# Hybrid stick-breaking and retention step: four raw operand buffers, three sum buffers, and x rows that wait for products

## The chip, the cores and the metric

One core of a Trainium2 chip runs the whole kernel. The metric is the device time of one execution in microseconds (us); the time of a kernel is the median of its runs. A core has five engines that each take their instructions in order: TensorE (PE, the matmuls), VectorE (DVE), ScalarE (ACT), GpSimd (POOL) and SyncE (SP). DMA transfers are issued from the queues of SP, ACT and POOL, and each issue, too, stands in its engine's order.

## The reference

One layer over 1024 prompt frames and 8 streams of 16 frames each, model width 2048, 8 + 8 heads of 128, in fp32. Cut to what matters:

```python
h = rms_norm(xp, norm_pre)
q_sb, k_sb, v_sb, gate_sb, q_r, k_r, v_r, gate_r = project(h, w_in, pos)   # 2048 -> 8 x 1024
o_sb = stick_breaking(q_sb, k_sb, v_sb)        # causal, per block of 128 queries
o_r, s = retention(q_r, k_r, v_r, s0, log_gamma)   # chunks of 64, carries a state
y = concat(head_rms_norm(o_sb, g_sb) * silu(gate_sb),
           head_rms_norm(o_r, g_r) * silu(gate_r))
out = einsum('bte,ed->btd', y, w_out)          # 2048 -> 2048
xp = xp + rms_norm(out, norm_post)
```

The sample streams run the same with 1024 cached frames of keys and values and a retention state. Returned are the new rows, the keys and values, and the states.

## The kernel before

Every fp32 operand is split into a high and a low part (`split`, L163 to L166: ACT writes the high part, L165, DVE the rest, L166), and every product is three matmuls: high by high, high by low, low by high. The names follow that: `mh`, `ml` for the moving operand, `wh`, `wl` for weights, `ah`, `al` for the left operands of the last stage; `mr`, `wr`, `yr`, `ys`, `br` are raw tiles that a DMA fills.

The 1024 + 128 frames are nine tiles of 128 rows in two groups. Group 0 has four prompt tiles and the sample (640 columns), group 1 the other four (512). The stages in order of time:

1. The normalized, transposed input `h` is made and written to memory (`s_h`) for group 1.
2. Group 0: per head the eight column panels of the input projection (L369, or L425 for the value rows), with stick-breaking attention and retention between them. The gated head outputs go to memory (`s_y`, L687).
3. The change of groups, about 1057 to 1104 us: `load_moving` (L243) reads group 1's operand from `s_h` block by block (16 blocks of 128 x 512, in quarters of four) through raw tiles `mr` and splits it. It is driven from the matmul loops of the last head of group 0 (`gates`, L1123, and `project_rows`, L403), which step it a quarter at a time, while the last attention of group 0 is still going on: `kp`, `kb` and `be` (L632, L633) are its sigmoids on ACT.
4. Group 1, the same, until about 1943 us. In the place of `load_moving`, `first_left` (L1032) reads the first left operands of the last stage from `s_y` and `s_s` through `mr`.
5. The output projection, as seven products of half-size matrices in a Strassen-like scheme (`product(n, nh, ...)`, L1188, matmuls L1162, L1165, L1166). Its left operands are rows of `y` (`s_y`) or sums of them (`s_s`), read by `left` (L293) and `left_sample` (L315); its right operands are blocks of `w_out` or sums of them (`s_b`), read by L1179. `sums` (L274) makes the sums: two loads fill a tile `br`, four DVE operations (L286) combine it, ACT's queue stores it (L289). Product (5, 0) of group 0 runs from 1943 us, product 1 from 1988, products 2, 5, 3, 6, 7 follow, then (4, 0).
6. The last product, (4, 1): `keep_blocks` (L1375) loads and splits all its weight blocks once; four tiles, `LAST`, are multiplied one after the other, normalized, added to the rows of x that `load_row` (L1336) has read, and stored (L1289).

What sets the order: matmuls are written out in sequence, and after each block `tick()` lets the jobs around it go a step. A `Job` is a generator; what it yields is the number of ticks until its next step (`D_MR`, `D_OP`, `D_SUM3` are such numbers). So the program's text and these numbers fix the order on every engine and queue. An instruction whose operand is not there holds up everything behind it on its engine. A raw tile with two buffers can be asked for again only after the split before the last has read it, and SP, which issues the load, waits for that, with all later loads behind it.

Of the kernel before, what the change touches and what calls it, by code (L numbers as in the profile page):

```python
# [11 lines left out]
F32 = mybir.dt.float32  # L12
# [47 lines left out]
D_MR = 6  # L60
D_OP = 2
D_SUM2 = (4, 6, 36)
D_SUM3 = (2, 3, 6)
LAG = 2
AHEAD = 2
HT = KT // 2
# [24 lines left out]
def tile_hybrid_step(  # L91
# [150 lines left out]

    def load_moving(mov, at, n, src):  # L243
        hi, lo = mov
        for k in range(KT):
            q, j = divmod(k, WQ)
            if q == len(hi):
                for x, y in zip(mov, moving_part(mp, NMAX, q)):
                    x.append(y)
            r = wp.tile([P, n], F32, name="mr", tag="mr", bufs=2)  # L250
            nc.sync.dma_start(r, src(k))
            split(hi[q][:, j, at : at + n], lo[q][:, j, at : at + n], r)
            yield D_MR

    def sum_weights(k, c):
# [15 lines left out]
        ops = ((3, 1, 3, "a"), (1, 0, 1, "s"), (0, 3, 0, "s"), (2, 2, 0, "s"))  # L271
        return load, ops, s_s[gi][h]

    def sums(pool, items, pace):  # L274

        def fetch(load):
            r = pool.tile([P, 4, 256], F32, name="br", tag="br", bufs=2)
            load(r)
            return r

        r = fetch(items[0][0])
        yield pace[2]
        for i, (_, ops, dst) in enumerate(items):
            nxt = fetch(items[i + 1][0]) if i + 1 < len(items) else None
            for o, a, b, how in ops:
                pin(nc.vector.tensor_tensor(r[:, o], r[:, a], r[:, b], ALU.add if how == "a" else ALU.subtract))  # L286
                yield pace[0]
            yield pace[1]
            pin(nc.scalar.dma_start(dst, r))  # L289
            r = nxt  # L290
            yield pace[2]
# [147 lines left out]
    with ExitStack() as s1:  # L439
# [592 lines left out]
        def first_left():  # L1032
            drain(summed[0])
            mine["s", 0] = [[half[h // WQ][:, h % WQ, NB_TOK:] for h in range(HT)] for half in mov]
            yield from left_sample(0, *mine["s", 0], wp, "mr", 2)
            mine[0, 5] = kept(0)
            yield from left(0, 5, *mine[0, 5], wp, "mr", 2)

        ret_job = sb_job = sub = loads = after = None
        for gi, g in enumerate(GROUPS):  # L1040
# [7 lines left out]
            for h in range(H):  # L1048
# [28 lines left out]
                def attention():  # L1077
                    nonlocal sb_job, sub, ip
                    acc = project(g, mov, col(0, h))
                    held = project(g, mov, col(1, h)) if h == H - 1 else None  # L1080
                    drain(sb_job)
                    if gi == 1 and h == 0:
                        drain(sub)
                        late.close()
                        banks.append(s1.enter_context(tc.tile_pool(name="psx", bufs=1, space=PSUM)))
                        ip = s1.enter_context(tc.tile_pool(name="ip2", bufs=1))
                        items = [sum_weights(k, c) for k in range(HT) for c in range(4)]
                        items[8:8] = [sum_rows(0, h) for h in range(H)]
                        summed.append(Job(sums(ip, items, D_SUM2), 8))
                        Job(residuals(), 150)  # L1090
                    q2 = [kq.tile([P, NB_TOK], F32R, name=f"q{c}", tag=f"q{c}") for c in "hl"]
                    evac_split(acc, *q2)
                    qs = None
                    if SAMPLE in tiles:
                        qs = kq.tile([P, P], F32, name="qs", tag="qs")
                        nc.scalar.activation(qs, acc[1][0][:, 2 * P : 3 * P], AF.Copy)
                    out = Out(4, "so")
                    rest = rows_in["sb"] = {}
                    if SAMPLE in tiles:
                        drain(sub)  # L1100
                        sub = Job(decode(h, qs, rest), D_DEC)
                    acc = held or project(g, mov, col(1, h))
                    kT = kq.tile([P, NMAX], F32, name="kT", tag="kT")
                    for a, (o, m) in acc:
                        nc.scalar.activation(kT[:, o : o + m], a[:, :m], AF.Copy)
                    pool, n = (ip, PT * P) if gi else (kq, NB_TOK)
                    k2 = [pool.tile([P, n], F32R, name=f"k{c}", tag=f"k{c}") for c in "hl"]
                    evac_split(acc, *k2, off * P)
                    if gi == 1:
                        kp = wp.tile([P, NB_TOK], F32, name="kpast", tag="mr", bufs=2)  # L1110
                        nc.sync.dma_start(kp, s_k[h])
                        split(k2[0][:, :NB_TOK], k2[1][:, :NB_TOK], kp)
                    rest["kT"] = kT
                    sb_job = Job(sb_branch(gi, g, h, out, q2, k2, kT, rest), D_NAT[phase[0]])
                    if h % 2 == 0:
                        pair["s"] = ep.tile([P, 8, 2, P], F32, name="vn", tag="vn")
                        project_rows(g, mov, col(2, h), pair["s"], off)
                    vn = pair["s"][:, :, h % 2, :]
                    if gi == 1:
                        nc.sync.dma_start(vn[:, :4, :], s_v[h])  # L1120
                    rest["vn"] = vn

                def gates():  # L1123
                    nonlocal after, loads
                    if h < H - 1:
                        rows_in["sb"]["sg"] = gate(project(g, mov, col(3, h)), "sg")
                        return

                    after = [[], []]
                    loads = first_left() if gi else load_moving(after, 0, NB_TOK, from_h)  # L1130
                    accs = project_pair(g, mov, (col(7, h), col(3, h)), loads)
                    rows_in["rest"]["rg"], rows_in["sb"]["sg"] = gate(accs[0], "rg"), gate(accs[1], "sg")

# [100 lines left out]
            outs[0, i] = mp.tile([P, WQ * NMAX], F32, name=t, tag=t)  # L1234
        Job(collect(5, 0, accs), 1)
        mine[0, 1] = kept(1)
        nxt = Job(left(0, 1, *mine[0, 1], wp, "mr", 2), D_OP)
        Job(collect(5, 1, product(5, 1, (0,), True, D_OUT)), 1)
        drain(nxt)
        drain(ret_job)  # L1240
# [4 lines left out]
    with ExitStack() as s3:  # L1245
# [68 lines left out]
        def both(n, groups):  # L1314
            made = []
            for g in groups:
                mine[g, n] = operand(c3, ("ah", "al"), 256, bufs=2) if g else kept(at[n])
                made.append(left(g, n, *mine[g, n], rp, f"yr{g}", 4))
            return made

        def jobs_of(made):
# [14 lines left out]
        def load_row(key):  # L1336
            i = LAST.index(key)
            pool, tag = ((xp[0], "x0"), (xp[0], "x1"), (rp, "out0"), (rp, "out1"))[i]
            rows[key] = pool.tile([P, D], F32, name=f"x{i}", tag=tag)
            pin(nc.sync.dma_start(rows[key], x_rows(tile_of((key[0], 2 + key[1])))))  # L1340

        def early_rows():
            for key in LAST[:2]:
# [1 line left out]
                yield 30  # L1345

        (first,) = both(1, G1)
        more = Job(sums(fp, [sum_rows(1, h) for h in range(H)], D_SUM3), 16)
        Job(load_gpost(), 40)
        ready = [Job(left_sample(1, *mine["s", 1], fp, "ys", 4), 24)]  # L1350
        for p in range(4):
# [23 lines left out]
        def keep_blocks():  # L1375
            for k in range(HT):
                wr = wp.tile([P, 512], F32, name="wr3", tag="wr", bufs=5)
                pin(nc.sync.dma_start(wr, weights_of(4, 1, k)))
                yield 1
                pin(*split(keep[0][k], keep[1][k], wr))  # L1380
                yield D_KEEP
            load_row(LAST[2])

        keeping = Job(keep_blocks(), 1)
        Job(collect(4, 0, product(4, 0, BOTH, False, 2)), 1)
# [1 line left out]
        scaled = [c3.tile([P, 2, 512], F32, name=f"og{t}", tag=t) for t in ("sh", "sl")]  # L1387
        for g, p in LAST:
            key = g, 2 + p
            if (g, p) == LAST[0]:  # L1390
                load_row(LAST[3])
            a = bank()
            for k in range(HT):
                times(a, mine[g, 4], k, TS[p], keep[0][k], keep[1][k], k == 0, k == HT - 1, k == 0)
                if (g, p) == (0, 0):
                    tick()
                    tick()
            if (g, p) == (0, 0):
                while jobs:
                    tick()  # L1400
            o = area(key, 1)
            nc.vector.tensor_tensor(o, o, a, ALU.subtract)
            square(key, 1, o)
            t = scaled[g][:, p, :]
            nc.vector.tensor_tensor(t, o, gpost[:, 512:1024], ALU.mult)
            rs = scale(key)
            for c in (0, 2, 3, 1):
                part = t if c == 1 else area(key, c)
                if c or (g, p) == (1, 1):
                    x = rows[g, p][:, c * 512 : (c + 1) * 512]  # L1410
                    nc.vector.scalar_tensor_tensor(part, part, rs, x, ALU.mult, ALU.add)
                    store(key, c, nc.sync, part)
                else:
                    nc.scalar.activation(part, part, AF.Copy, scale=rs)
                    add_out(key, c)
# [104 lines left out]
```

## Time and profile before

| | us |
|---|---|
| median of 3 runs | 2318.3 |
| lowest, highest | 2317.97, 2323.03 |
| profiled execution, its time | 2318.99 |
| profiled execution, span from first to last instruction | 2317.3 |
| PE busy | 2265.7 (98%) |
| DVE busy | 1231.3 (53%) |
| ACT busy | 919.1 (40%) |
| POOL busy | 358.1 (15%) |
| mean share of DMA engines of the three largest queues | 44.6%, 12.1%, 11.8% |

The granted clock of PE is 0.994 of full speed over the span. A row of a timeline has the start in us, the duration in us, the engine, the line of the kernel, the operation, output and inputs with their shapes, and in brackets how long the engine was idle before it, with what ended the idle time. An x2 or x3 behind a row joins equal instructions that follow each other. Matmuls are pipelined: the duration of one is longer than the distance to the next, and the distance tells the speed.

### The profile page before, as it was taken

The numbers are of one execution on the slowest core, as the hardware profiler recorded it, in microseconds if no ns is written. First come the engines' busy times: TensorE is split into PE (matmuls) and PEld (weight loads), VectorE is DVE, ScalarE is ACT, GpSimd is POOL, SyncE is SP. The second block draws the span as 40 slices with busy tenths as digits, with TensorE's granted clock in tenths as the row PEclk, the third lists the DMA queues.
The fourth block names the chain that finished last, engine by engine and source line by source line (L and its number), as shares of the span: only waits on it lengthen the run. The fifth ranks groups of instructions, "written<-read, shape, count | busy, mean of one in ns | idle before, by whom it ended". The sixth has DMA issues, their size and how long they took to land.

```text
span 2317.3 us, 39306 instructions
## 1 busy us (share of the span) xinstructions
PE 2265.7 (98%) x14496; PEld 2046.9 (88%) x14496; DVE 1231.3 (53%) x2541; ACT 919.1 (40%) x1951; POOL 358.1 (15%) x601
## 2 busy tenths in 40 slices
PE   7999999999999999999999999999999999899997
PEld 7999999999999999998888989898888887788886
DVE  7234444354534445355556565655665666546566
ACT  6323333333333333334433433343443445435363
POOL 3002020120202021111102111120211212000020
PEclk9999999999999999999999999999999999999999
DMA  7547657575566657568768777778787767755596
GB/s 257 180 144 201 190 152 218 173 196 186 150 194 198 195 158 231 168 187 254 192 205 233 216 210 236 214 229 230 221 231 216 212 169 182 247 191 183 148 210 177
DMA packets 446497, 462.61 MB, mean 200 GB/s; under 512 B 181984, under 2 KB 309984, under 8 KB 444640
## 3 DMA queue, kind: packets, MB, share of 16 engines
q1 hardware_dynamic: 315952, 295.69, 44.6%
q0 software_dynamic: 28720, 78.41, 12.1%
q10 hardware_dynamic: 101632, 86.00, 11.8%
q8 instruction: 113, 1.85, 0.3%
q14 instruction: 80, 0.66, 0.1%
HBM read 355.12 MB, written 114.29 MB: 203 GB/s over the span
## 4 chain that ended last, share of the span: by engine, by line
PE 85%; DMA 7%; DVE 4%; issue 2%; ACT 2%; SPq 0%; POOL 0%; DVEq 0%; ACTq 0%; POOLq 0%
PE acc L369 46%; PE accn L425 17%; PE a L1166 4%; PE a L1162 4%; PE a L1165 4%; PE pa L750 2%; PE z L720 2%; PE zc L789 1%; PE pd L853 1%; DMA mr<-s_h 1%; DMA s_o<-so 1%; PE pa L898 1%; DVE ml L166 1%; PE pS L913 1%; PE rs L880 1%
## 5 line engine op out<-in xcount | busy, mean ns | idle before, releaser
L369 PE MATMUL acc<-mh,wh 128*128 128x256 f32 (+2 forms) x2304 | 662.6, 340 | 0.0
L369 PE MATMUL acc<-ml,wh 128*128 128x256 f32 (+2 forms) x2304 | 659.0, 339 | 0.0
L369 PE MATMUL acc<-mh,wl 128*128 128x256 f32 (+2 forms) x2304 | 656.6, 338 | 0.0
L166 DVE TENSOR_TENSOR wl<-wr,wh 128x512 fp32r<-128x512 f32 x504 | 346.3, 690 | 495.3 <-ACT wh L165 475.9
L165 ACT ACTIVATE wh<-wr 128x512 fp32r<-128x512 f32 x504 | 317.0, 630 | 653.3 <-PE acc L369 341.1
L369 PEld LDWEIGHTS acc<-ml,wh 128*128 128x128 f32 x2304 | 421.6, 188 | 31.3 <-issue 3.3
L369 PEld LDWEIGHTS acc<-mh,wl 128*128 128x128 f32 x2304 | 424.2, 188 | 27.8
L369 PEld LDWEIGHTS acc<-mh,wh 128*128 128x128 f32 x2304 | 420.1, 188 | 31.9 <-issue 3.3
L425 PE MATMUL accn<-whn,mh 128*128 128x256 f32 x1152 | 330.4, 287 | 0.6 <-DVE rg L452 0.6
L425 PE MATMUL accn<-wln,mh 128*128 128x256 f32 x1152 | 326.4, 283 | 0.0
L425 PE MATMUL accn<-whn,ml 128*128 128x256 f32 x1152 | 326.0, 283 | 0.0
L425 PEld LDWEIGHTS accn<-whn,mh 128*128 128x128 f32 x1152 | 221.4, 192 | 4.0 <-issue 1.1
L425 PEld LDWEIGHTS accn<-wln,mh 128*128 128x128 f32 x1152 | 221.4, 192 | 0.8
L425 PEld LDWEIGHTS accn<-whn,ml 128*128 128x128 f32 x1152 | 221.1, 192 | 0.0
L166 DVE TENSOR_TENSOR wln<-wrn,whn 128x512 fp32r<-128x512 f32 x128 | 87.6, 687 | 147.0 <-ACT whn L165 146.6
L165 ACT ACTIVATE whn<-wrn 128x512 fp32r<-128x512 f32 x128 | 80.6, 633 | 187.7 <-PE accn L425 83.2
L613 POOL DMA_DIRECT2D be<-s_be x128 | 94.2, 742 | 149.8 <-DMA s_be<-be 126.9
L649 DVE TENSOR_TENSOR_SCAN kp<-kp 128x1152 f32<-128x1152 f32 (+4 forms) x40 | 82.8, 2069 | 52.1 <-POOL kp L638 35.4
L638 POOL TENSOR_SCALAR_AFFINE_SELECT kb<-kb 128x128 f32<-128x128 f32 x64 | 30.6, 485 | 459.2 <-ACT kb L632 456.9
L776 POOL DMA_DIRECT2D kcT<-cache_k x64 | 34.6, 545 | 423.6 <-PE pd L853 268.8
L1162 PE MATMUL a<-wh,mh 128*128 128x512 f32 x240 | 94.0, 393 | 2.6 <-ACT wh L165 1.9
L1166 PE MATMUL a<-wh,ml 128*128 128x512 f32 x240 | 94.0, 392 | 0.0
(259 smaller groups left out, 3008.9 us busy)
## 6 DMA issues: line engine op xcount, KB each, us to landing
wr<-w_cols SPq DMA_DIRECT2D x384, 256.0 KB, 4.4
wrn<-w_rows SPq DMA_DIRECT2D x128, 256.0 KB, 3.6
kcT<-cache_k POOLq DMA_DIRECT2D x64, 512.0 KB, 8.2
vc<-cache_v SPq DMA_DIRECT2D x64, 512.0 KB, 5.9
wr<-s_b SPq DMA_DIRECT2D x80, 256.0 KB, 4.2
br<-w_out SPq DMA_DIRECT2D x64, 256.0 KB, 5.0
s_b<-br ACTq DMA_DIRECT2D x32, 512.0 KB, 4.8
wr<-w_out SPq DMA_DIRECT2D x48, 256.0 KB, 3.9
```

The costliest lines, as they stand in the source:

```text
L165: nc.scalar.activation(hi, src, AF.Copy),
L166: nc.vector.tensor_tensor(lo, src, hi.bitcast(F32), ALU.subtract),
L369: last = nc.tensor.matmul(a[:, :m], lhs[:, j, :], rhs[w][:, j, o : o + m], start=(w == 0 and j == 0 and n == 0), stop=(w == KT // WQ - 1 a ...
L425: anchor[0] = nc.tensor.matmul(a, lhs[q][:, jj, ts], rhs[:, j, :], start=(w == 0 and j == 0 and n == 0 and t % 2 == 0), stop=(w == KT // 2 ...
L613: q.dma_start(raw[32 * i : 32 * i + 32, :].rearrange("p (k a) -> p k a", a=32), s[:, :, 32 * i : 32 * i + 32].rearrange("k (j b) a -> b (k ...
L649: nc.vector.tensor_tensor_scan(rev, rev, rev, 1.0, ALU.mult, ALU.bypass)
L720: nc.tensor.matmul(z[:, :c], q2[a][:, i * P : (i + 1) * P], k2[b][:, s : s + c], start=(m == 0), stop=(m == 2),)
L750: nc.tensor.matmul(po[:, :P], at[:, j, :], vn[:, j, :], start=(j == 0), stop=(j == t))
L776: ready.append((kc, nc.gpsimd.dma_start(kc, cache_k[h, m // 4, m % 4])))
L1162: ins = nc.tensor.matmul(a, hi[k][:, ts], wh, start=first, stop=False)
L1165: nc.tensor.matmul(a, hi[k][:, ts], wl, start=False, stop=False)
L1166: anchor[0] = nc.tensor.matmul(a, lo[k][:, ts], wh, start=False, stop=last)
```

## The change

1. Raw `mr` tiles have four buffers (`MR`) instead of two. `load_moving` asks for four blocks first, and for block k + 4 after the split of block k; at the change to group 1 the first four are asked for before the last pair of projections begins. `first_left`, the past keys (`kpast`) and the operand of product (0, 1) use four buffers as well.
2. In the last stage, the left operands of group 0 pass through `mr` instead of a tile `yr0` of their own; those of group 1 keep theirs, now called `yr`.
3. `sums` takes its number of buffers: two for the sums of weights, as before, and three for the sums of group 1's rows. Those start 30 ticks into the last stage instead of 16, and their first pace is 3 instead of 2.
4. `load_row` for the last two rows of x moves from the end of `keep_blocks` and the first of the four tiles to the tiles (0, 0) and (0, 1), and waits for the last product matmul written before it.

```diff
-D_SUM3 = (2, 3, 6)
+D_SUM3 = (3, 3, 6)
+MR = 4
@@ load_moving
+        raw = []
+
+        def load(k):
+            r = wp.tile([P, n], F32, name="mr", tag="mr", bufs=MR)
+            nc.sync.dma_start(r, src(k))
+            raw.append(r)
+
+        for k in range(MR):
+            load(k)
+        yield D_MR
         for k in range(KT):
...
-            r = wp.tile([P, n], F32, name="mr", tag="mr", bufs=2)
-            nc.sync.dma_start(r, src(k))
-            split(hi[q][:, j, at : at + n], lo[q][:, j, at : at + n], r)
+            split(hi[q][:, j, at : at + n], lo[q][:, j, at : at + n], raw.pop(0))
+            if k + MR < KT:
+                load(k + MR)
             yield D_MR
@@ sums
-    def sums(pool, items, pace):
+    def sums(pool, items, pace, bufs):
-            r = pool.tile([P, 4, 256], F32, name="br", tag="br", bufs=2)
+            r = pool.tile([P, 4, 256], F32, name="br", tag="br", bufs=bufs)
@@ first_left
-            yield from left_sample(0, *mine["s", 0], wp, "mr", 2)
+            yield from left_sample(0, *mine["s", 0], wp, "mr", MR)
-            yield from left(0, 5, *mine[0, 5], wp, "mr", 2)
+            yield from left(0, 5, *mine[0, 5], wp, "mr", MR)
@@ sums of the weights
-                        summed.append(Job(sums(ip, items, D_SUM2), 8))
+                        summed.append(Job(sums(ip, items, D_SUM2, 2), 8))
@@ attention
-                        kp = wp.tile([P, NB_TOK], F32, name="kpast", tag="mr", bufs=2)
+                        kp = wp.tile([P, NB_TOK], F32, name="kpast", tag="mr", bufs=MR)
@@ gates
                     loads = first_left() if gi else load_moving(after, 0, NB_TOK, from_h)
+                    if gi == 0:
+                        next(loads)
@@ product (0, 1)
-        nxt = Job(left(0, 1, *mine[0, 1], wp, "mr", 2), D_OP)
+        nxt = Job(left(0, 1, *mine[0, 1], wp, "mr", MR), D_OP)
@@ both
-                made.append(left(g, n, *mine[g, n], rp, f"yr{g}", 4))
+                made.append(left(g, n, *mine[g, n], *((rp, "yr", 4) if g else (wp, "mr", MR))))
@@ load_row
-            pin(nc.sync.dma_start(rows[key], x_rows(tile_of((key[0], 2 + key[1])))))
+            load = nc.sync.dma_start(rows[key], x_rows(tile_of((key[0], 2 + key[1]))))
+            pin(load)
+            if i > 1:
+                tc.add_manual_dep(
+                    load.ins,
+                    anchor[0].ins.name,
+                    mybir.DependencyInfo(mybir.DependencyClass.Sync, mybir.DependencyReason.DATA),
+                    reason="behind the weights",
+                )
@@ sums of group 1's rows
-        more = Job(sums(fp, [sum_rows(1, h) for h in range(H)], D_SUM3), 16)
+        more = Job(sums(fp, [sum_rows(1, h) for h in range(H)], D_SUM3, 3), 30)
@@ keep_blocks
-            load_row(LAST[2])
@@ the last four tiles
-            if (g, p) == LAST[0]:
-                load_row(LAST[3])
+            if g == 0:
+                load_row((1, p))
```

The diff's lines shift those of the functions behind by up to 21: `split` is at L166 and L167, the first stage of `kp` and `be` at L643 and L644.

Three places of the order of instructions. First ACT at the change of groups, the last two quarters of group 1's operand (`mh<-mr`) beside the projection's weights (`whn<-wrn`), the gates (`rg`, `sg`) and the last attention's sigmoids (`kp`, `be`, `kb`). Before:

```order
L165 ACTIVATE mh_12331<-mr 128x512 x2
L165 ACTIVATE whn<-wrn 128x512
L451 ACTIVATE sg<-acc_11996 128x256
L451 ACTIVATE sg<-acc_11997 128x384
L165 ACTIVATE mh_12430<-mr 128x512
L632 ACTIVATE kp<-zc 128x512
L165 ACTIVATE mh_12430<-mr 128x512
L633 ACTIVATE be<-zc 128x512
```

and with the change:

```order
L166 ACTIVATE whn<-wrn 128x512
L462 ACTIVATE sg<-acc_12004 128x256
L462 ACTIVATE sg<-acc_12005 128x384
L166 ACTIVATE mh_12438<-mr 128x512 x4
L643 ACTIVATE kp<-zc 128x512
L644 ACTIVATE be<-zc 128x512
```

Before, a split of the last quarter stands ahead of `kp` and another between `kp` and `be`; the last two come later. With the change all four stand ahead of `kp`, and `be` follows `kp`.

Second DVE in product 1 of the last stage: the last splits of its left operand (`al<-yr`) among splits of weights (`wl<-wr`) and the sums (`br<-br`; the number names the tile, so 21574 is the third sum and 21628 the fourth before, 21552 the second and 21620 the third after). Before:

```order
L286 TENSOR_TENSOR br_21574<-br_21574 128x256
L166 TENSOR_TENSOR wl3_21583<-wr3_21580,wh3_21582 128x512
L166 TENSOR_TENSOR al_21407<-yr1_21495,ah_21406 128x256
L286 TENSOR_TENSOR br_21574<-br_21574 128x256 x2
L166 TENSOR_TENSOR al_21407<-yr1_21545,ah_21406 128x256
L166 TENSOR_TENSOR wl3_21613<-wr3_21610,wh3_21612 128x512
L286 TENSOR_TENSOR br_21574<-br_21574 128x256
```
```order
L286 TENSOR_TENSOR br_21628<-br_21628 128x256
L166 TENSOR_TENSOR wl3_21643<-wr3_21640,wh3_21642 128x512
L166 TENSOR_TENSOR al_21407<-yr1_21586,ah_21406 128x256
```

and with the change:

```order
L297 TENSOR_TENSOR br_21552<-br_21552 128x256
L167 TENSOR_TENSOR al_21407<-yr_21534,ah_21406 128x256
L167 TENSOR_TENSOR wl3_21605<-wr3_21602,wh3_21604 128x512
L297 TENSOR_TENSOR br_21552<-br_21552 128x256 x2
```
```order
L167 TENSOR_TENSOR al_21407<-yr_21578,ah_21406 128x256
L167 TENSOR_TENSOR wl3_21634<-wr3_21631,wh3_21633 128x512
L297 TENSOR_TENSOR br_21620<-br_21620 128x256
```

The last `al` stood behind the first operation of the fourth sum, and now stands behind the second sum and ahead of the third.

Third SP at the end of product (4, 0), with the x rows and the last weight blocks (`wr<-s_b`, L1179 for (4, 0) and L1378 for the last product). Before:

```order
L1179 DMA wr_24111<-s_b_6_109 128x512
L1378 DMA wr_24125<-s_b_7_118 128x512
L1340 DMA x_24132<-x_prompt 128x2048
L1179 DMA wr_24137<-s_b_7_110 128x512
L1340 DMA x_24181<-x_prompt 128x2048
L1289 DMA out<-mh_21215 128x512 x2
```

and with the change, with the waits that the instructions carry (the number behind an engine's name is only a semaphore's):

```order
L1399 DMA wr_24125<-s_b_7_118 128x512 [waits DMAHW5_49,DVE_49]
L1192 DMA wr_24135<-s_b_7_110 128x512 [waits DMAHW6_49,DVE_49]
L1353 DMA x_24179<-x_prompt 128x2048 [waits DMASW2_49,DMASW1_49,DMASW3_49,DMASW0_49,PE_49]
L1353 DMA x_24246<-x_prompt 128x2048 [waits DMASW6_49,DMASW5_49,DMASW7_49,DMASW4_49,PE_49]
L1302 DMA out<-mh_21215 128x512 [waits DVE_49]
```

The last weight block of (4, 0) now stands ahead of both x rows, and both x rows wait for PE.

## The prediction

> **What bounds the kernel now.** I read the page first, then the timeline of TensorE (PE) for its gaps, then the engine or queue that ended each gap.
>
> ```profile
> span 2317.3 us, 39306 instructions
> PE 2265.7 (98%) x14496; PEld 2046.9 (88%) x14496; DVE 1231.3 (53%) x2541; ACT 919.1 (40%) x1951; POOL 358.1 (15%) x601
> ```
>
> PE works 2265.7 of 2317.3 us. The change takes no matmul away, so it can only touch the 51.6 us in which PE stands still, and the stretches in which the matmuls run at half speed. Five places are within its reach. The first is the change of groups; PE's timeline, then ACT's:
>
> ```profile
> 1097.13 1.51 PE L978 MATMUL pSs<-rv,rkn 32*128 32x128 f32 x3 [3.39 <-ACT be L633]
> ...
> 1099.46 0.58 PE L425 MATMUL accn<-whn,mh 128*128 128x256 f32 x1
> 1099.84 0.41 PE L425 MATMUL accn<-wln,mh 128*128 128x256 f32 x1
> 1100.05 0.41 PE L425 MATMUL accn<-whn,ml 128*128 128x256 f32 x1
> ...
> 1103.46 0.29 PE L425 MATMUL accn<-whn,mh 128*128 128x256 f32 x1
> 1103.59 0.28 PE L425 MATMUL accn<-wln,mh 128*128 128x256 f32 x1
> ```
> ```profile
> 1093.36 0.63 ACT L165 ACTIVATE mh<-mr 128x512 fp32r<-128x512 f32 x1 [2.73 <-DMA mr<-s_h]
> 1093.90 0.58 ACT L632 ACTIVATE kp<-zc 128x512 f32<-128x512 f32 x1
> 1095.96 0.63 ACT L165 ACTIVATE mh<-mr 128x512 fp32r<-128x512 f32 x1 [1.49 <-DMA mr<-s_h]
> 1096.50 0.58 ACT L633 ACTIVATE be<-zc 128x512 f32<-128x512 f32 x1
> ```
>
> PE waits for be, and be stands on ACT behind two splits of group 1's operand, each waiting for its raw block. Then the matmuls follow each other every 0.21 us until 1103.46, and every 0.13 us after: the clock is halved for a while.
>
> The second place is the start of the last stage's product 1 (PE, ACT, then the DMA issues of two short windows), the third the same product 27 us later (PE, DVE, and SP's waits):
>
> ```profile
> 1988.07 0.80 PE L1162 MATMUL a<-wh,ah 128*128 128x512 f32 x1 [2.64 <-ACT ah L165]
> ...
> 1990.80 0.46 PE L1162 MATMUL a<-wh,mh 128*128 128x512 f32 x1
> ```
> ```profile
> 1982.48 0.35 ACTq L687 DMA_DIRECT2D s_y<-sg  x1
> 1987.60 1.03 ACT L165 ACTIVATE ah<-yr 128x256 fp32r<-128x256 f32 x3 [5.93 <-DMA br<-s_y]
> ```
> ```profile
> br<-s_y SPq DMA_DIRECT2D x2, 256.0 KB, 5.3
> s_y<-sg ACTq DMA_DIRECT2D x1, 256.0 KB, 4.9
> ```
> ```profile
> out<-mh SPq DMA_DIRECT2D x2, 256.0 KB, 2.6
> ```
> ```profile
> 2014.74 0.73 PE L1166 MATMUL a<-wh,al 128*128 128x512 f32 x1 [3.66 <-DVE al L166]
> 2015.27 0.63 PE L1165 MATMUL a<-wl,ah 128*128 128x512 f32 x1
> 2015.70 0.63 PE L1166 MATMUL a<-wh,al 128*128 128x512 f32 x1
> ...
> 2018.26 0.39 PE L1165 MATMUL a<-wl,mh 128*128 128x512 f32 x1
> 2018.49 0.39 PE L1166 MATMUL a<-wh,ml 128*128 128x512 f32 x1
> ```
> ```profile
> 2013.32 0.43 DVE L286 TENSOR_TENSOR br<-br 128x256 f32<-128x256 f32 x1 [4.74 <-DMA br<-s_y]
> ...
> 2014.27 0.42 DVE L166 TENSOR_TENSOR al<-yr,ah 128x256 fp32r<-128x256 f32 x1
> ```
> ```profile
> SPq L269 <- DMA s_s<-br: 9.6, 3, 4.1
> ```
>
> In the second, the first ah starts 0.18 us after the store s_y<-sg (issued at 1982.48, 4.9 us) has landed at 1987.4; the page names a br load, which landed later than ah started, so I take the store for the releaser. In the third DVE stands at a sum whose operand has not arrived, and al, ready, is queued behind it. The br load was itself late: SP held three of them 9.6 us until an older sum was stored, as there are two buffers. Both gaps are followed by matmuls 0.43 us apart instead of 0.23.
>
> The fourth place is the end of product (4,0): PE, SP's issues, and the landing times of the four x rows (min/median/max), with the page's row for the weights:
>
> ```profile
> 2282.56 0.73 PE L1162 MATMUL a<-wh,mh 128*128 128x512 f32 x2 [1.87 <-ACT wh L165]
> ...
> 2283.60 0.39 PE L1165 MATMUL a<-wl,mh 128*128 128x512 f32 x1
> ...
> 2285.87 0.39 PE L1166 MATMUL a<-mh,ml 128*128 128x512 f32 x1
> ```
> ```profile
> 2272.74 0.33 SPq L1340 DMA_DIRECT2D x<-x_prompt  x1
> 2273.16 0.38 SPq L1179 DMA_DIRECT2D wr<-s_b  x1
> ```
> ```profile
> DMA to landing us min/median/max: 8.4/9.4/10.6
> ```
> ```profile
> wr<-s_b SPq DMA_DIRECT2D x80, 256.0 KB, 4.2
> ```
>
> The last weight block is asked for behind a 1-MB row of x. The fifth is the end of group 1, three small gaps:
>
> ```profile
> 1931.27 0.49 PE L913 MATMUL pS<-rv,rkn 128*128 128x128 f32 x2 [0.90 <-DVE rkn L1003]
> 1938.95 0.49 PE L898 MATMUL pa<-rv,sc 128*128 128x128 f32 x2 [0.60 <-DVE ro L907]
> 1942.94 0.50 PE L1162 MATMUL a<-wh,mh 128*128 128x512 f32 x1 [0.72 <-DVE rg L452]
> ```
>
> **The change part by part.** No engine gets more or fewer operations, apart from the two waits of the x rows.
>
> *Four raw buffers, change of groups.* In the new order ACT has all four splits of the last quarter, then kp and be. The two waits ahead of be (2.73 and 1.49, 4.2 us) go if the four blocks are asked for a quarter ahead; two more splits, 2 x 0.63, come in front. So be starts 4.2 - 1.3 = 2.9 us earlier, which leaves 0.5 of the 3.39 us. A gap so short leaves the clock alone, I take it: from 1099.46 to 1103.46 are 19 matmuls 0.21 apart, at 0.13 or a little less 2.4 us, so 1.6 us come back. The short matmuls at 1097.13 to 1099.46 ran at half speed too; between 0 and half of 2.3 us comes back there, I take 0.8. Together 2.9 + 1.6 + 0.8 = **5.3 us**; at most 3.39 + 1.6 + 1.1 = 6.1, at least 2 if the loads in fours land together and late.
>
> *Same buffers, end of group 1.* The splits that stood between the parts of the retention chain no longer wait for pairs; the weights of the next product are asked for a few us later. Of 0.90 + 0.60 + 0.72 = 2.2 us I take **0.9**, ends -1 and 2.2.
>
> *Sums start later, the start of product 1.* The four br loads after the store's issue now come behind the sample's loads, so the store shares the DMA engines with less. Its time lies between 2.6 us (a 256-KB store into quiet) and today's 4.9; I take 3.6, nearer the middle because two weight loads remain. That is 1.3 us of the 2.64. The slow stretch behind it, six matmuls in 2.73 us instead of 6 x 0.23 = 1.4, costs 1.3 more; half a chance that it goes, 0.7. Together **2.0 us**, ends 0 and 4.0. The ACT queue now has the store of the head's other output behind the splits of the raw blocks; DVE's work ahead of sg gives that store about 2 us of cover, and what it is late beyond that would be paid here in full.
>
> [...]
>
> *Three buffers for the sums, the gap at 2014.74.* A br load no longer waits for the store of the sum just before, and in the new order of DVE the eighth al stands ahead of the third pair's sums. The gap of 3.66 and eight matmuls in 3.52 us instead of 8 x 0.23 = 1.84 make 3.66 + 1.7 = 5.4 us. The eighth yr load is now behind all the sample's loads and the second pair on SP; a block 1 us late is my guess between 0 and 2.4. So **4.4 us**, ends 3 and 5.4.
>
> *The x rows.* With the row behind it, the last weight block takes x2's place at 2272.74 and lands 4.2 us later, near 2277; PE wanted it at 2280.7. The gap goes, **1.9 us**. x2 is now asked for when the last product matmul of (4,0) has ended, about 2286, x3 after the first of the four last tiles, 8 blocks of 3 matmuls at 0.23 = 5.5 us later, about 2291.5. At 10.6 us, the longest of the four, they land at 2296.6 and 2302.1.
>
> ```profile
> 2305.14 1.42 DVE L1411 SCALAR_TENSOR_TENSOR out<-out,outr,x 128x512 f32<-128x512 f32 x2
> ```
>
> x2 is first read at 2305.1, x3 a tile later, some 5.5 us: 8 us of cover for each. Behind the waiting loads SP has only the output stores. If the cover failed, each us over it would be added to the end.
>
> *Not seen in the trace:* waits that the new order of SP makes elsewhere, from 0 to 3 us; I take 0.5.
>
> Sum: 5.3 + 0.9 + 2.0 + 4.4 + 1.9 - 0.5 = **14.0 us**. The profiled execution took 2318.99 us, 1.7 more than its span and 0.7 more than the median of the runs, 2318.3. From the profiled one it is 2305.0, from the median **2304.3**, which I forecast. With all the good ends, 6.1 + 2.2 + 4.0 + 5.4 + 1.9 = 19.6, it is 2298.7; with the bad, 2 - 1 + 0 + 3 + 1.9 - 3 = 2.9, it is 2315.4. Its own likely range is 2299 to 2310.
>
> **The rivals.**
>
> *The DMA engines are the bound in product 1.* Window 2000 to 2050 (busy PE, PEld, DVE, ACT, POOL, granted clock, DMA share, GB/s):
>
> ```profile
> 2000.00:2050.00 50.00, 46.13 (x195) 37.38 (x194) 27.69 (x66) 21.84 (x47) 0.00 (x0) 0.97 0.77 253
> ```
>
> If PE's 3.87 idle us vanish, the same bytes need 0.77 x 50 / 46.1 = 0.83 of the engines: there is room on the mean, but loads asked for in bursts may wait for each other. Then the second and third place keep their gaps in another form: 14.0 - 6.4 = 7.6, 2310.7. [...]
>
> *The clock stays halved.* Shorter gaps still trip it: of the terms above 1.6 + 0.8 + 0.7 + 1.7 = 4.8 are clock. 14.0 - 4.8 = 9.2, 2309.1. For it speaks the half speed after only 2.64 us, against it the full speed after 1.87 us at 2282.56 (the matmul at 2283.60 takes 0.39 us, not 0.63).
>
> *Slower: four raw loads in front of the weights.* At the change of groups SP asks for four blocks in a row and, being in order, waits on the raw buffers with the next wrn load behind it. A weight block that is asked for too late costs its landing, 3.6 us,
>
> ```profile
> wrn<-w_rows SPq DMA_DIRECT2D x128, 256.0 KB, 3.6
> ```
>
> its split, 1.3 us, and a stretch at half speed, 1.7: 6.6 us for each quarter. The first term turns from 5.3 to -6.6 times the quarters. One gives 2318.3 - 8.7 + 6.6 = 2316.2, two 2322.8: it decides from the second on, four would be 2336. Against it: weight blocks have five buffers, so that their loads stand ahead of their use, and today's pairs wait in the same queue without a gap of PE that a weight block ends there.
>
> *It does not do what it says.* If the loads come no earlier because the buffers are freed as late as before, it stays near 2318.3. The new order, with splits in fours and the weight ahead of the x row, speaks against it.
>
> **How the numbers follow.** Forecast 0.60, DMA bound 0.17, clock 0.15, slower 0.05, nothing 0.03. The first three are nearly all gains; a measurement of this kernel tells a change from none at about 0.2%, 4.6 us, and a tenth of those cases falls inside that or is eaten by waits I do not see. That gives faster 0.87, same 0.08, slower 0.05. The range must reach to the two milder rivals with some spread and to the sum's good end: 2298 to 2312.
>
> **What would show it.** Right: ACT's kp and be next to each other at the change of groups and no PE gap over 1 us there; no gap at the eighth al of product 1; no gap before (4,0)'s last block, and x rows landing before their readers; PE busy within 1% of 2265.7 or a little less, as slow matmuls go. Wrong: a PE gap over 2 us released by a weight block (whn or wh) at the change of groups; ah at the start of product 1 still 2.6 us late or later; DMA share above 0.9 around 2000 us with gaps released by yr or wr loads; a longer tail after the last matmul, waiting for x.

## The result and the profile after

The changed kernel takes 2303.5 us, median of six runs (2301.4 to 2307.5), against 2318.0 us before (2316.6 to 2323.0): ratio 0.9937, 95% interval 0.9924 to 0.9949. That is 14.5 us less; forecast were 14.0, and 2304.3 us. The profiled execution took 2303.65 us, with a span of 2301.9.

The page of the changed kernel: PE does the same matmuls and stands still 40.2 us instead of 51.6; 4 us of its busy time are gone as well, as fewer matmuls run slowly (granted clock 0.996 over the span, 0.994 before).

```profile
span 2301.9 us, 39303 instructions
PE 2261.7 (98%) x14496; PEld 2045.1 (89%) x14496; DVE 1231.9 (54%) x2541; ACT 919.7 (40%) x1951; POOL 356.8 (16%) x601
```

Where the time came from shows best when the same matmul is looked up in both timelines of PE (start times in us):

| matmul | before | after | after - before |
|---|---|---|---|
| in the last head of group 0, ahead of the change of groups | 1054.40 | 1056.06 | +1.7 |
| behind the change of groups | 1104.18 | 1098.09 | -6.1 |
| in the middle of group 1 | 1589.11 | 1582.49 | -6.6 |
| at the end of group 1 | 1945.11 | 1940.57 | -4.5 |
| behind the first blocks of product 1 | 1991.56 | 1984.13 | -7.4 |
| behind the eighth al of product 1 | 2020.32 | 2007.12 | -13.2 |
| last ones of product (4, 0) | 2285.42 | 2270.05 | -15.4 |
| last of all | 2306.95 | 2291.58 | -15.4 |

So the steps are: change of groups -7.8, end of group 1 +2.1, start of product 1 -2.9, eighth al -5.8, (4, 0) -2.2, between them -0.5, tail 0. The +1.7 at the top lies in a part that the change does not touch: over the 14 profiles of this document that matmul starts from 1.9 us earlier to 4.2 us later than in the kernel before. So the total of one execution is good to some 3 us, and a step is as firm as it repeats. The step at the change of groups does: it is -7.8 in all ten profiles with four raw buffers, and between +0.1 and +0.5 in the other three. The one at the end of group 1 keeps its sign, but lies between +0.2 and +2.7 in the six profiles with the same code there, mostly by whether half speed follows the gap. And a run that leaves product 1 as it was (x rows alone, below) has gaps of 3.50 and 1.99 us where the kernel before has 2.64 and 3.66.

*Change of groups.* ACT, then PE:

```profile
1089.07 2.19 ACT L166 ACTIVATE mh<-mr 128x512 fp32r<-128x512 f32 x4
1091.14 0.59 ACT L643 ACTIVATE kp<-zc 128x512 f32<-128x512 f32 x1
1091.62 0.60 ACT L644 ACTIVATE be<-zc 128x512 f32<-128x512 f32 x1
```
```profile
1094.25 0.28 PE L436 MATMUL accn<-whn,ml 128*128 128x256 f32 x1
1094.46 0.38 PE L989 MATMUL pSs<-rv,rkn 32*128 32x128 f32 x2
...
1095.12 0.38 PE L436 MATMUL accn<-whn,mh 128*128 128x256 f32 x1
1095.34 0.28 PE L436 MATMUL accn<-wln,mh 128*128 128x256 f32 x1
1095.46 0.28 PE L436 MATMUL accn<-whn,ml 128*128 128x256 f32 x1
```

The four splits run in one piece without a wait, be ends at 1092.2, and PE arrives at pSs 2.2 us later. No gap, and matmuls 0.12 us apart right behind.

*End of group 1.* Here a gap has grown. PE, DVE and ACT:

```profile
1932.01 0.49 PE L909 MATMUL pa<-rv,sc 128*128 128x128 f32 x2 [2.05 <-DVE so L764]
...
1934.92 0.63 PE L380 MATMUL acc<-ml,wh 128*128 128x512 f32 x1
1935.35 0.63 PE L380 MATMUL acc<-mh,wl 128*128 128x512 f32 x1
```
```profile
1930.12 0.42 DVE L167 TENSOR_TENSOR ml<-mr,mh 128x256 fp32r<-128x256 f32 x1 [2.20 <-ACT mh L166]
1930.72 0.43 DVE L167 TENSOR_TENSOR ml<-mr,mh 128x256 fp32r<-128x256 f32 x1 [0.17 <-ACT mh L166]
1931.07 0.68 DVE L167 TENSOR_TENSOR wl<-wr,wh 128x512 fp32r<-128x512 f32 x1
1931.67 0.28 DVE L764 COPY so<-pa 128x128 f32<-128x128 f32 x1
```
```profile
1929.67 0.42 ACT L166 ACTIVATE mh<-mr 128x256 fp32r<-128x256 f32 x1 [2.93 <-DMA mr<-s_s]
```

PE waits for the copy so; so stands on DVE behind two splits of the first left operand of product (5, 0), and these wait for a raw block. Before, so was ahead of them (DVE, kernel before):

```profile
1935.90 0.28 DVE L753 COPY so<-pa 128x128 f32<-128x128 f32 x1
...
1938.20 0.42 DVE L166 TENSOR_TENSOR ml<-mr,mh 128x256 fp32r<-128x256 f32 x1 [1.83 <-ACT mh L165]
```

*Product 1.* Its start (PE, then ACT), and the 50 us behind it:

```profile
1982.18 0.50 PE L1175 MATMUL a<-wh,ah 128*128 128x512 f32 x1 [1.10 <-ACT ah L166]
1982.51 0.40 PE L1178 MATMUL a<-wl,ah 128*128 128x512 f32 x1
```
```profile
1977.90 0.33 ACTq L698 DMA_DIRECT2D s_y<-sg  x1
1981.71 1.03 ACT L166 ACTIVATE ah<-yr 128x256 fp32r<-128x256 f32 x3 [5.23 <-DMA s_y<-sg]
```
```profile
2000.00:2050.00 50.00, 50.00 (x223) 41.40 (x222) 25.87 (x56) 20.05 (x41) 0.00 (x0) 1.00 0.78 259
```

The page itself now names the store s_y<-sg as what ah waits for. 1.1 us of the 2.64 are left, at full speed; and from 2000 to 2050 PE has no idle time, with the DMA engines at 0.78.

*The x rows.* SP's issues, and the landing of the first of the two late rows:

```profile
2260.11 0.32 SPq L1192 DMA_DIRECT2D wr<-s_b  x1
2270.24 5.77 SPq L1353 DMA_DIRECT2D x<-x_prompt  x2
```
```profile
x<-x_prompt SPq DMA_DIRECT2D x1, 1024.0 KB, 5.0
```

The last weights are asked for 10 us before the first row is asked for; that row lands 5.0 us later, at 2275.3, and its reader on DVE comes at 2289.75.

### The profile page after: what moved, and what is told of

It is laid out like the page before. It is cut to its first block, busy times and chain, and to the rows that moved or that the text cites. A ratio compares the mean times of both kernels' runs of the same rounds, so it can differ in the third digit from the quotient of the medians.

```text
span 2301.9 us, 39303 instructions
## 1 busy us (share of the span) xinstructions
PE 2261.7 (98%) x14496; PEld 2045.1 (89%) x14496; DVE 1231.9 (54%) x2541; ACT 919.7 (40%) x1951; POOL 356.8 (16%) x601
## 4 chain that ended last, share of the span: by engine, by line
PE 87%; DMA 6%; DVE 4%; issue 1%; ACT 1%; SPq 1%; POOL 0%; DVEq 0%; ACTq 0%; POOLq 0%
PE acc L380 45%; PE accn L436 17%; PE a L1178 5%; PE a L1179 5%; PE a L1175 5%; PE z L731 2%; PE pa L761 2%; PE zc L800 1%; DMA s_o<-so 1%; PE pd L864 1%; DMA ro<-s_rk 1%; PE pa L909 1%; DMA dT<-c_dt 1%; PE pS L924 1%; DMA s_rk<-rk 1%
## 5 line engine op out<-in xcount | busy, mean ns | idle before, releaser
L167 DVE TENSOR_TENSOR wl<-wr,wh 128x512 fp32r<-128x512 f32 x504 | 346.4, 690 | 497.5 <-ACT wh L166 477.9
L166 ACT ACTIVATE wh<-wr 128x512 fp32r<-128x512 f32 x504 | 317.3, 631 | 654.2 <-PE acc L380 341.8
L167 DVE TENSOR_TENSOR wln<-wrn,whn 128x512 fp32r<-128x512 f32 x128 | 87.8, 688 | 152.4 <-ACT whn L166 151.1
L166 ACT ACTIVATE whn<-wrn 128x512 fp32r<-128x512 f32 x128 | 80.7, 633 | 192.9 <-PE accn L436 86.9
L1178 PE MATMUL a<-wl,mh 128*128 128x512 f32 x240 | 93.5, 390 | 0.0
L1179 PE MATMUL a<-wh,ml 128*128 128x512 f32 x240 | 93.6, 390 | 0.0
```

What stands on the lines that cost most here:

```text
L166: nc.scalar.activation(hi, src, AF.Copy),
L167: nc.vector.tensor_tensor(lo, src, hi.bitcast(F32), ALU.subtract),
L1178: nc.tensor.matmul(a, hi[k][:, ts], wl, start=False, stop=False)
L1179: anchor[0] = nc.tensor.matmul(a, lo[k][:, ts], wh, start=False, stop=last)
```

## The experiments

Twelve runs in three groups, each group on one chip: ten new kernels, the changed kernel once more, and one of the ten once more. The ratio is always to the kernel before on the same chip, in the same group.

**One part alone.** Three kernels are the kernel before with one part of the change each. The raw buffers go together with part 2 of the change, which takes away the tile `yr0`.

> The kernel before with the four raw buffers alone (and the left operands of group 0 passing through them, without which the memory does not suffice); sums and x rows as before. Theory (each part is worth what the trace of the changed kernel shows at its own place): the change of groups alone gains 7.8 us and the end of group 1 loses 1.8; the gaps of 2.64, 3.66 and 1.87 us in the last stage stay. Time 2318.0 - 6 = 2312.0. Rival (raw buffers also shorten the gaps of product 1, by freeing SP): below 2309. Rival (the group change's gain is paid back in the last stage): 2316 to 2318.

Measured: ratio 0.9967 (0.9955 to 0.9980), 2310.3 against 2318.2 us. At the change of groups there is no gap, at the end of group 1 one of 2.82 us, at the start of product 1 one of 1.97 us, and at the eighth al

```profile
2002.55 0.50 PE L1179 MATMUL a<-wh,al 128*128 128x512 f32 x1 [0.73 <-DVE al L167]
```

where the kernel before had 3.66. The gaps in product 1 do shrink, so the first rival is half right, though two new ones (1.17 and 0.60 us, for weights) stand beside them. The gap in (4, 0), with the x rows where they were, is 1.16 us here instead of 1.87.

```diff
-D_SUM3 = (2, 3, 6)
+D_SUM3 = (3, 3, 6)
-            r = pool.tile([P, 4, 256], F32, name="br", tag="br", bufs=2)
+            r = pool.tile([P, 4, 256], F32, name="br", tag="br", bufs=bufs)
-        more = Job(sums(fp, [sum_rows(1, h) for h in range(H)], D_SUM3), 16)
+        more = Job(sums(fp, [sum_rows(1, h) for h in range(H)], D_SUM3, 3), 30)
```

> The kernel before with the sums alone changed (three buffers, start at 30 ticks, pace 3). Theory: the gap of 3.66 us at the eighth al of product 1 with its slow stretch goes, 5.8 us, and most of the gap at the start of product 1, 2.9 us; change of groups as before. Time 2318.0 - 8.7 = 2309.3. Rival (the gap at the start of product 1 was shortened by the raw buffers, not by the later start of the sums): gap of 2.6 us stays there, 2312.2.

Measured: 0.9967 (0.9953 to 0.9980), 2310.3 us. The gap at the eighth al is gone, the one at the start of product 1 is not. Its row on PE, and the DMA issues of the 7 us around the store:

```profile
1985.41 0.50 PE L1162 MATMUL a<-wh,ah 128*128 128x512 f32 x1 [3.24 <-ACT ah L165]
```
```profile
wr<-w_out SPq DMA_DIRECT2D x3, 256.0 KB, 5.5
s_y<-sg ACTq DMA_DIRECT2D x1, 256.0 KB, 5.6
```

No br load is near, and yet the store takes 5.6 us: three weight loads went out in the 1.2 us ahead of it. By the gap the rival holds; the time lies between the two, 2309.3 and 2312.2, and does not tell them apart. Fewer br loads did not help it: in the kernel before, with two br loads issued right behind it, it took 4.9 us.

> The kernel before with only the x rows moved behind the last weights. Theory: the gap of 1.87 us in (4,0) goes, nothing else, time 2318.0 - 2.0 = 2316.0, last matmul and tail as far apart as before. Rival (the late rows make the tail longer, hidden in the changed kernel by nothing): tail longer by over 1 us, 2318 or more.

Measured: 0.9992 (0.9981 to 1.0002), 2316.5 us; the gap in (4, 0) is gone, and from the last matmul to the end it is as far as before. As the theory has it, though a part so small is not clear of no change in the times alone.

The three parts give 3.3 + 3.3 + 0.8 = 7.4 thousandths, all together 6.3. An overlap is to be expected, since both of the larger parts cure the eighth al; but each ratio is only good to about 1.2 thousandths, so the 1.1 between the two sums do not show it.

**The end of group 1.** First the lead of the loads, one block instead of three:

```diff
-        for h in range(deep - 1):
+        for h in range(lead):
             load(h)
...
-            yield from left(0, 5, *mine[0, 5], wp, "mr", MR)
+            yield from left(0, 5, *mine[0, 5], wp, "mr", MR, 1)
```

> The changed kernel, but the first left operands of the last stage (at the end of group 1) are asked for one block ahead, as before, not three; buffers stay four. Theory (three blocks asked for at once meet the weight loads and their splits hold up DVE in front of the copy so that PE waits for): the gap of 2.05 us at 1932 goes back to about 0.6, its slow stretch goes, 2 to 3 us faster than the changed kernel, near 2301. Rival (the gap is from the place of the splits in DVE's order and not from the lead): gap stays at 1.5 us or more, 2303 to 2304. Rival (the first operands come late without the lead and product (5,0) waits): slower, over 2305.

Measured: 0.9923 (0.9897 to 0.9949), 2298.9 us. The time came out near the expected one, though with four runs the ratio is not clear of the changed kernel's, and the reason did not: the gap is still there.

```profile
1926.65 0.49 PE L909 MATMUL pa<-rv,sc 128*128 128x128 f32 x2 [2.48 <-DVE so L764]
...
1927.43 0.39 PE L380 MATMUL acc<-mh,wl 128*128 128x512 f32 x1
```
```profile
1925.37 0.43 DVE L167 TENSOR_TENSOR ml<-mr,mh 128x256 fp32r<-128x256 f32 x1 [1.24 <-ACT mh L166]
1925.71 0.68 DVE L167 TENSOR_TENSOR wl<-wr,wh 128x512 fp32r<-128x512 f32 x1
1926.31 0.28 DVE L764 COPY so<-pa 128x128 f32<-128x128 f32 x1
```

The lead is not it; the splits still stand ahead of so. Against the changed kernel its profile wins 1.4 us at the start of product 1, where the gap went to nothing, since the store s_y<-sg was issued 4.9 us ahead of PE's last matmul instead of 2.8, and 1.2 us at the end of group 1, where no half speed follows the gap this time. So the next one moves the splits and leaves the loads where they are:

```diff
-            yield from left(0, 5, *mine[0, 5], wp, "mr", MR)
+            steps = left(0, 5, *mine[0, 5], wp, "mr", MR)
+            yield next(steps)
+            yield D_MR
+            yield D_MR
+            yield from steps
```

> The changed kernel, but the first left operand of product (5,0) is split two steps later: its loads are asked for as early as before, and on DVE its first two splits stand behind the copy (so) that PE waits for, where they stood ahead of it. Theory (with the lead ruled out, it is the place of these two splits that makes the gap at the end of group 1): the gap of 2.05 us goes back to 0.3 to 0.6, 1.5 to 3 us faster than the changed kernel, 2301 to 2302. Rival (the splits are needed early; the gap moves to the first matmul of product (5,0)): a new gap of 1 us or more there, 2303 to 2305.

Measured: 0.9908 (0.9892 to 0.9925), 2299.5 us on a chip on which the kernel before took 2321.8. The gap in front of pa is gone. A shorter one appears at product (5, 0), and at the start of product 1 the first ah is on time; PE, then ACT:

```profile
1934.86 0.50 PE L1179 MATMUL a<-wh,mh 128*128 128x512 f32 x1 [1.14 <-ACT mh L166]
```
```profile
1968.57 0.33 ACTq L698 DMA_DIRECT2D s_y<-sg  x1
...
1973.01 1.04 ACT L166 ACTIVATE ah<-yr 128x256 fp32r<-128x256 f32 x3
```

Both the theory and its rival's gap came true, the sum on the theory's side. As the changed kernel was not in that group, the third runs it, this one and a step between them side by side (the one between has one `yield D_MR` instead of two).

> The changed kernel once more, on the chip of the three runs beside it, so that they can be compared with it. Theory: the ratio to the kernel before is 0.9937 again, within 0.9924 and 0.9949; gaps of 1.5 to 3 us at the end of group 1 (in front of pa, released by so) and 0.7 to 1.5 us at the start of product 1, none at the eighth al, none in (4,0).

> The changed kernel with the splits for product (5,0) two steps later, once more, beside the changed kernel itself. Theory: no gap in front of pa, a gap of about 1.1 us at the first matmuls of product (5,0), none at the start of product 1; 3 to 5 us faster than the changed kernel on this chip. Rival (its lead in the earlier run was the chip and the execution): within 2 us of it.

> The same with one step instead of two: on DVE one of the two splits stands ahead of the copy so, the other behind. Theory (each split ahead of so makes it wait for its own raw block): the gap in front of pa is between that of the changed kernel and none, 1 to 2 us, the time between the two, 1 to 2.5 us faster than the changed kernel. Rival (one split ahead waits as long as two, since their blocks land 0.4 us apart): gap 2 us or more, no faster than the changed kernel.

| kernel | ratio to before (95%) | median us | gap in front of pa |
|---|---|---|---|
| changed | 0.9933 (0.9915 to 0.9951) | 2304.5 | 2.44 |
| one step later | 0.9918 (0.9901 to 0.9934) | 2301.8 | 2.30 |
| two steps later | 0.9906 (0.9890 to 0.9922) | 2298.6 | none |

The changed kernel repeats its ratio. With two steps it is 5.9 us faster in the medians, more than its gaps account for: 2.4 and some 1.7 for the slow stretch behind, less the new 1.1, and the 1.3 at the start of product 1 make 4.3. The intervals overlap, so the size is not settled; but all six runs of it (2295.5 to 2302.6) lie below all six of the changed kernel (2302.8 to 2309.5). It has the lowest ratio here. With one step the rival is right about the gap, one split ahead costs as much as two. Where the 2.7 us of its median come from stays open: at the start of product 1, where it has no gap, its profile wins 1.0 us on the changed kernel beside it, but from the first to the last row of the table of matmuls above it wins 14.9 us on the kernel before, and the changed kernel 15.7.

**The sums of rows.** Three kernels take the part apart.

> The changed kernel with two buffers for the sums of rows; they still start at 30 ticks with pace 3. Theory (the third buffer is what keeps DVE from standing at a sum with the eighth al behind it): the gap at the eighth al comes back, 1 to 3.7 us, with up to 1.7 us of slow matmuls; 2305 to 2308. Rival (the later start alone puts al ahead of the sums, and the raw buffers free SP): no gap over 0.3 us there, 2303.5.

Measured: 0.9919 (0.9903 to 0.9935), 2303.8 us. The rival is right, from the start of product 1 PE stands still for 0.04 us in 50:

```profile
1980.00:2030.00 50.00, 49.96 (x220) 40.87 (x220) 30.29 (x72) 24.86 (x55) 0.00 (x0) 1.00 0.89 290
```

> The kernel before with only the start of the sums of rows moved from 16 to 30 ticks; two buffers and pace 2 stay. Theory (the later start puts the eighth al ahead of the third sum, and that, not the third buffer, ends the gap there): no gap over 0.5 us at the eighth al, ratio to before 0.996 to 0.998, as with all three edits of the sums, 0.9967. Rival (without raw buffers the third buffer is needed): a gap of 1 us or more at an al of product 1, ratio 0.998 or more.

Measured: 0.9977 (0.9963 to 0.9991), 2315.0 us. With two buffers, pace 2 and no raw buffers the gap at the eighth al is gone all the same:

```profile
1992.00:2030.00 38.00, 38.00 (x169) 31.41 (x168) 21.63 (x54) 17.86 (x44) 0.00 (x0) 1.00 0.90 292
```

It keeps the gap at the start of product 1 (3.23 us), and has two small ones 43 and 57 us into product 1, 0.38 and 0.54 us, for weights. No kernel with three buffers has these, but neither has the run just above, with two and with raw buffers. So what the third buffer is worth stays open; it is not needed to end the gap that the prediction gave it.

> The changed kernel with the sums of rows started at 16 ticks with pace 2, three buffers. Theory of the prediction (the later start keeps br loads away from the store that the first ah waits for): the gap at the start of product 1 grows from 1.1 to 2 us or more, 2305. Rival (which the run with the sums alone speaks for: the gap there was 3.2 us although no br load shared with the store): the gap stays near 1 us, 2303 to 2304, since what the store meets are the weight loads.

Measured: 0.9932 (0.9917 to 0.9946), 2305.0 us. Here the prediction's own theory holds: with the br loads back beside the store, the gap is what it was. (The ratio alone does not show it; it is the changed kernel's.) PE, and the issues of the 5 us behind the store:

```profile
1980.94 0.80 PE L1175 MATMUL a<-wh,ah 128*128 128x512 f32 x1 [2.60 <-ACT ah L166]
```
```profile
br<-s_y SPq DMA_DIRECT2D x2, 256.0 KB, 5.2
wr<-w_out SPq DMA_DIRECT2D x1, 256.0 KB, 4.9
s_y<-sg ACTq DMA_DIRECT2D x1, 256.0 KB, 5.0
```

At the eighth al this kernel has no gap either, though the sums start as early as before: with raw buffers and two sum buffers it was 0.73 us (the first run), with three it is none. Together with the run of the sums alone: the store took 5.0 us beside two br loads, 5.6 beside three weight loads, and 3.5 in the changed kernel (1977.90), where one weight load went out 0.7 us ahead of it and the next load of SP 4.7 us behind it. The later start takes the br loads away there, and in the 1.2 us ahead of the store one weight load goes out, not three.

**The wait of the x rows.**

```diff
             pin(load)
-            if i > 1:
-                tc.add_manual_dep(
...
-                )
```

> The changed kernel without the wait of the last two x rows for the product; their place in SP's order stays, behind the last weight block. Theory (the order alone gives the 1.9 us): the last weight block lands a little later, 5 to 6 us instead of 4.2, still ahead of its use; no gap in (4,0) or at most 0.5 us, 2303 to 2304. Rival (the wait is needed, as the row, issued 0.4 us after, shares all engines with the block): the gap comes back to 1 us or more, 2304.5 to 2305.5.

Measured: 0.9917 (0.9902 to 0.9931), 2302.6 us. No gap in (4, 0). The slowest of the last weight loads took 5.5 us (min/median/max of the three in 2257 to 2263),

```profile
DMA to landing us min/median/max: 3.6/4.2/5.5
```

and was in time. As far as this can tell, the place in the queue is the whole effect, and the wait adds nothing to it.

## Why the prediction was right, point by point

- **Change of groups, 5.3 forecast, 7.8 found.** The mechanism is as described, the term too small. The gap of 3.39 us went whole, not but for 0.5, because the third quarter's splits, too, ran without waiting: sg, behind them on ACT, ended 2.2 us earlier against PE. The short matmuls around pSs took 0.7 us (1094.46 to 1095.12) instead of 2.3 (1097.13 to 1099.46): 1.7, where I had taken 0.8 and called 1.1 the most; half speed was not all that had held them, as the kb behind be on ACT was late too (a pSs on PE started only when it was done, at 1098.06). And a gap of 0.61 us at 1087, behind the same splits, had been left out.
- **End of group 1, +0.9 forecast as a gain, 2.1 lost.** Here the step failed, in its sign: "The splits that stood between the parts of the retention chain no longer wait for pairs". The buffers also let the splits of (5, 0) move ahead of so, and there they wait for blocks that are still on the way: a new gap of 2.05 us and a slow stretch, 1.7 us. With the splits two steps later the gap is gone, which shows the cause. DVE's order would have shown the move beforehand.
- **Start of product 1, 2.0 forecast, 2.9 found.** The gap shrank by 1.5 us (1.3 forecast) and its slow stretch went whole (0.7 taken for half a chance). The cause holds only in company: with the sums alone the store met weights, 5.6 us; with raw buffers and the early start it met br loads, 5.0 us; with both parts it took 3.5 us, and 3.6 had been taken. The page's wrong name for the releaser before, a br load, is set right by the page after.
- **Eighth al, 4.4 forecast, 5.8 found.** The 5.4 us of the gap and its slow stretch went, with 0.2 of a small one ahead. The 1.0 us for a late yr block was not needed. But the reason named first, "A br load no longer waits for the store of the sum just before", is not needed: with two buffers the gap is gone as well, in two kernels. The second, that al stands ahead of the third sum, is enough, and that is the later start's doing. It is not the only cure: raw buffers alone shorten the gap to 0.73 us, and raw buffers with three sum buffers end it even with the early start. No run has the third buffer alone.
- **x rows, 1.9 forecast, 2.2 found.** Right in place and price. The cover was larger than worked out, since the rows took 5.0 us each with no load beside them, not 10.6. The price may be a little high: the gap is 1.87 us in the kernel before, and 0.9 to 1.2 in the three other kernels that leave the x rows as they were.
- **The rivals.** DMA as the bound in product 1 fell: PE is busy for all of 2000 to 2050 with the DMA share at 0.78; other kernels ran with 0.04 us of idle time or none at 0.89 and 0.90. The clock fell in four of the five places; it is halved, for 3.41 us, behind the new gap at 1932. Weights behind raw loads did not occur: no gap at the change of groups at all. Nor did the blocks come as late as before: the last four are split in one piece.

The total is right partly by luck. The steps found, 0.5 between them included, add up to 17.1 us, not 14.0: too little had been taken at the change of groups (2.5), the start of product 1 (0.9), the eighth al (1.4) and the x rows (0.3), and 1.0 for unseen waits, 0.5 taken off where 0.5 was won; too much at the end of group 1 (3.0). That the two profiles differ by only 15.4 us comes from the 1.7 of the table's first row, which is chance; the medians differ by 14.5. The chances do not follow from their own words, either: the first three make 0.92, and less a tenth that is 0.83 for faster, not 0.87.

## What to carry to other kernels

More buffers on a tile did two things here: loads started earlier (the 4.2 us that ACT waited ahead of be are gone), and what uses the tile moved ahead of other work on DVE (so, behind two splits, with a gap of 2.05 us on PE); look for what now stands behind it. A wait in front of one instruction was cured by the order alone, at the last block of (4, 0) (1.87 us before, none without the semaphore) and at the eighth al (3.66 us before, none with the later start alone), so try the move before the buffer or the semaphore. And a store that the next stage waits for should be issued when the load queues are quiet: here the same 256 KB took from 2.0 us, with no other load issued in the 1.8 us on either side (two steps later, second run), to 5.8 us, with two weight and two br loads issued within 1.3 us (x rows alone).

## What the runs showed of the hardware

The slow stretches behind gaps of PE. In the 14 profiles (kernels before and changed, and the twelve runs) there are 146 gaps of PE over 0.7 us behind the first 60 us. The trace's clock record says whether the clock drops to half within the next 5 us. It did so behind 23 of them: 16 of the 28 from 1.8 to 3.3 us, and all 7 from 3.39 us up; the other 111, from 0.7 to 1.75 us, were followed by full speed. A slow stretch lasted 3.41 us, or, behind 5 of the 7, 6.83, and began 2 to 4.5 us behind the start of the gap. In the kernel before, 3.41 us at half speed followed the gaps of 1.91 (at 1271), 2.64 and 3.66 us, 6.83 us the one of 3.39, and none the one of 1.87; in the changed kernel 3.41 us followed the gaps of 2.33 (at 1265) and 2.05. The shortest gap with half speed behind it has 1.80 us:

```profile
657.63 0.49 PE L909 MATMUL pa<-rv,sc 128*128 128x128 f32 x2 [1.80 <-DVE sc L893]
...
659.29 0.73 PE L380 MATMUL acc<-ml,wh 128*128 128x256 f32 x2
659.82 0.74 PE L380 MATMUL acc<-mh,wl 128*128 128x256 f32 x2
```

(the changed kernel's second profile; two matmuls take 0.46 us there at full speed). One of 3.24 us had none behind it (the row at 1985.41 above, whose next matmuls take 0.40 us). So among the gaps of 1.8 to 3.3 us the length alone did not tell which of them half speed follows. What does, and why five stretches lasted twice the time, no run was made to show.

Half of the time that PE worked in such a stretch was lost: 1.4 to 1.7 us in one of 3.41 us, 2.9 to 3.4 in one of 6.83. An estimate for these kernels from those counts: a gap costs itself and, where half speed follows, some 1.7 us more, or some 3 where it lasts 6.83.
